# The last block of a mixture-of-experts layer is added by a gate matrix on TensorE instead of through DRAM

## The chip, the cores and the metric

One core of a Trainium2 chip runs the whole program. The metric is the device time of one execution in microseconds (us); lower is better. The engines are TensorE (PE), VectorE (DVE), ScalarE (ACT), GpSimd (POOL) and SyncE (SP); each takes its own instructions in order. Data between DRAM and on-chip memory moves through 16 DMA engines, which serve queues that SP, ACT and POOL issue to.

## The reference, cut to what matters

The program computes a block with four mixers and a dense feed-forward part, and behind it two layers, numbered 0 and 1 here. Each layer is a mixer, a layer norm, a mixture of experts and another layer norm. There are 32 experts of width 512 over 1024 features, and each token (512, in layer 0 with two more) takes its two best. The kernel's two steps behind the experts are

```python
gates = pg * jax.nn.softmax(vals, axis=-1)          # two gates for a token
...
xs = xpad[slot_tok].reshape(n_blocks, BLK, D)        # blocks of tokens of one expert
def expert_block(args):
    xb, e = args
    hb = jax.nn.silu(xb @ w_gate[e]) * (xb @ w_up[e])
    return hb @ w_down[e]
...
y = jnp.zeros((T + 1, D)).at[slot_tok].add(ys * slot_gate[:, None])
...
h = layer_norm(ALPHA * h + y, ln_g, ln_b)
```

## The kernel before

Each layer's mixture runs in one function. It routes the tokens, gathers them by expert from DRAM, and then takes 16 steps `u`, each a block of 128 rows that holds two experts (a pair). A step is `gate_up` (the two input products `peg`, then SiLU on ACT and a product on DVE), `hpose` (four transposes `pex` and a DVE copy), `down` (the output products `pey0`, `pey1`), and `scatter` (two ACT copies `eys<-pey`, then an indirect DMA from POOL that writes each row to the place of its token and choice in the DRAM array `dy`). `ORDER` is the order of the blocks; its last is block 15.

The experts' weights, 6 MB for an expert, are a stream: SP issues 1 MB DMAs into a ring of buffers `sr` as they come free. `items_moe` lays down their order. Behind one step's gate and up weights stand the down weights of the step before it, and the last step's down weights come at the very end: [gate and up of 15] [down of 14] [down of 15].

Behind the last step ACT scales the residual rows `xt` (in layer 0 also the two rows `hm`) by `ALPHA` (L2387). A loop for overfull experts follows (L2390); it has no rounds here, but all engines meet there. Then SP reads `dy` back by token (`cy<-dy`, 4 MB, L2418). The `COMBINE` string gives the order of the steps by token tile: S adds the two choices times their gates (two DVE instructions of 128x1024, L294 and L2423), N is the layer norm, G gain and bias (POOL L1620 and DVE L1621), T transposes the tile for the next mixer. In layer 0 the products `pl` of the short-convolution mixer follow; its weights `sc_w_in` are each split in two parts (ACT L222, DVE L224) in buffers `sh_*`. In layer 1 the tiles go to the output.

The order within each engine's queue around the experts is settled by a scheduler from the program, not by the text's order alone; the COMBINE part is under a manual order.

Of the kernel before, what the change touches and what calls it, by code (L numbers as in the profile page):

```python
# [46 lines left out]
NB = (NP + MORE + 1) // 2 * 2  # L47
CT = 32
GPC = ((640, 448, 640, 384, 448), (832, 832, 512, 320))
COMBINE = ("M4 S0 S1 N0 N1 S2 S4 N4 G0 G1 G4 T0 T1 T4 S3 N2 G2 N3 G3", "S0 S1 N0 S2 N1 S3 N2 G0 G1 N3 G2 G3")  # L50
MOE_W = ("moe_w_gate_2", "moe_w_up_2", "moe_w_down_2")
EPS = 1e-6
LN_EPS = 1e-5
# [1790 lines left out]
def items_moe(e, l):  # L1844


    def own(x):
        return lambda i: e.I[MOE_W[i]][l][x]

    def ranked(r):  # L1850
        return chosen(e, l, lambda: e.ranked(r))

    e.moe_first[l] = len(e.st.items)
    last = []
    for u in ORDER:
        pair = [own(x) for x in STAT[u]] if u < NST else [ranked(u), ranked(NE - 1 - u)]
        it = [p_ for pp in zip(*(expert_items(w) for w in pair)) for p_ in pp]
        n = len(it) * 2 // 3
        for i in it[:n] + last:
            e.st.add(*i)  # L1860
        last = it[n:]
    for i in last:
        e.st.add(*i)
# [168 lines left out]
def moe(e, mo):  # L2032
# [10 lines left out]
    with ExitStack() as ph:  # L2043
# [2 lines left out]
        xg = [sp.tile([P, D], F32, name=f"xg{i}") for i in range(2)]  # L2046
        for x_ in xg:
            G.memset(x_, 0.0)
        def small(name, shape, dt=F32):
            return sp.tile([P] + list(shape), dt, name=name)  # L2050

# [167 lines left out]
                                  q + k == 0, q + k == 2)  # L2219
            return pp  # L2220

        def scatter(po, yi):
            if not ysb:
                y2 = sp.tile([P, 2 * D], F32, name="eys")
                ysb.extend((y2[:, :D], y2[:, D:]))
            ys = ysb[0]
            ysb.rotate(1)
            for h in range(2):
                e.late = A.copy(ys[:, h * 512:(h + 1) * 512], po[h])  # L2229
            G.indirect_dma_start(out=dy[:, :], out_offset=bass.IndirectOffsetOnAxis(ap=yi, axis=0), in_=ys, in_offset=None,  # L2230
                                 bounds_check=2 * n_tok - 1, oob_is_err=False)

        def gates():

# [48 lines left out]
            V.tensor_copy(lst[:, :NL], pc_[:, 16:16 + NL])  # L2283
            V.tensor_copy(nov, pc_[:, 8:9])

        def block():

            b0 = sp.tile([P, 2], I32, name="ob0")
            ts(b0[:, 0:1], lst[:, 0:1], NE - 1, op0=OP.bitwise_and)
            ts(b0[:, 1:2], lst[:, 0:1], 5, op0=OP.arith_shift_right)  # L2290
            bf_ = sp.tile([P, 2], F32, name="obf")
            V.tensor_copy(bf_, b0)
            eo = sp.tile([P, NE], F32, name="oeo")
            ts(eo, mo.io, bf_[:, 0:1], op0=OP.is_equal)
# [21 lines left out]
            return ev, ox, oy  # L2316

        NL = 16
        gt = mo.gt
# [47 lines left out]
        def scatters(u, pp):  # L2367
            for b_, po in zip(work[u], pp):
                scatter(po, yix[:, b_:b_ + 1])

        get = lambda: st.raw_get(2)
        for u in range(NP):
            sg = gate_up(xs, get)
            if u + 1 < NP:
                xs = next_x(u + 1)
            if hs is not None:
                scatters(u - 1, down(hs, get))
            if u == 4:
                rows = mo.gain_bias(gb, l * 2 + 1)
                g, b = next(rows)  # L2380
            if u == NP - 2:
                next(rows)
            hs = [(hpose(x_), cut) for x_, cut in sg]
        scatters(NP - 1, down(hs, get))
        with tc.issue_after(e.late.ins):
            for h, n in rows_:
                A.activation(h, h, AF.Copy, scale=ALPHA)  # L2387
        if e.overflow:
            nv = nc.values_load(nov[0:1, 0:1], min_val=0, max_val=NL)
            with tc.For_i(0, nv, 1) as _:  # L2390
                ev, ox, oy = block()
# [9 lines left out]
                scatter(po, oy)  # L2401

    e.left = []
    if l == 0:
        e.xm.__exit__(None, None, None)
        e.act3 = tc.tile_pool(name="act3", bufs=1, side="right", reuse_waits="tile")
        e.open_act(e.act3.__enter__())
    with tc.tile_pool(name=f"cb{l}", bufs=1, reuse_waits="tile") as sp:
        order = [NT, 0, 1, 2, 3] if l == 0 else range(NT)
        ys = {}  # L2410
        with tc.manual_schedule(engines={mybir.EngineType.SP}):
            for t in order:
                if l == 0 and t == NT - 1:
                    st.stop()
                    st.prefetch()
                n = rows_[t][1]
                ys[t] = sp.tile([P, 2, D], F32, name="cy", bufs=4)
                Q.dma_start(ys[t][:n], dy[2 * t * P:2 * (t * P + n), :].rearrange("(t k) c -> t k c", k=2))  # L2418
        def sums(h, n, t):
            y_ = ys[t][:n]  # L2420
            stt(h, y_[:, 0, :], gt[:n, t, 0:1], h, OP.mult, OP.add)
            sm = sp.tile([P, 1], F32, name="csum", bufs=4)[:n]
            V.scalar_tensor_tensor(h, y_[:, 1, :], gt[:n, t, 1:2], h, op0=OP.mult, op1=OP.add, accum_out=sm)  # L2423
            return ln_sums(e, sp, h, n, [sm], y_[:, 0, :])

        def scaled(h, n, t):

            y_ = ys[t][:n]
            for k in range(2):
                A.activation(y_[:, k, :], y_[:, k, :], AF.Copy, scale=gt[:n, t, k:k + 1])  # L2430
                G.tensor_tensor(h, h, y_[:, k, :], op=OP.add)
            yield
            sm = sp.tile([P, 1], F32, name="msum")[:n]
            A.activation(y_[:, 0, :], h, AF.Identity, accum_out=sm)
            yield ln_sums(e, sp, h, n, [sm], y_[:, 0, :], "m")

        def step(c, t):
            h, n = rows_[t]
            if c == "M":
                ms[t] = scaled(h, n, t)  # L2440
                next(ms[t])
            elif c == "S":
                ms[t] = next(ms[t]) if t == NT else sums(h, n, t)
            elif c == "N":
                ln_norm(e, sp, h, n, *ms[t], "m" if t == NT else "")
            elif c == "G":
                ln_gain(e, h, n, g, b, GPC[l][t])
                if l == 1:
                    Q.dma_start(e.out[0, t * P:(t + 1) * P, :], h)
            else:  # L2450
                e.tile_to_fm(h, 2 + t * P if t < NT else 0, n)

        ms = {}
        with tc.manual_schedule(engines={mybir.EngineType.DVE, mybir.EngineType.Activation, mybir.EngineType.Pool}):
            t = order[0]
# [40 lines left out]
```

## Time and profile before

| | us |
|---|---|
| median of 3 runs | 2580.27 (2578.97 to 2581.33) |
| the profiled execution | 2577.17 |
| its span, first to last instruction | 2575.1 |

Times in the trace are microseconds from the start of the span. Layer 0's expert steps end with the last `pey` product at 1763.25, those of layer 1 at 2525.10. A row of a timeline has the start, the duration, the engine, the line and the operation, `out<-in`, how many were put together, and in brackets how long the engine had been idle and what ended that.

### The profile page before, as it was taken

Reading aid. Unit: us, or ns where it says so; the run is one execution under the profiler, and the core shown is the slowest. Engines: PE = TensorE matmul, PEld = TensorE weight load, DVE = VectorE, ACT = ScalarE, POOL = GpSimd, SP = SyncE. Lnnn points to the kernel's source line nnn. Section 1 sums busy time; section 2 is a strip of 40 time slices with the busy share of each in tenths; the row PEclk is TensorE's granted clock in tenths of the full one; section 3 lists DMA queues with packets and bytes.
Section 4 is the critical chain, followed back from the end, with each engine's and each line's share of the span. In section 5 each row is a group of like instructions: output and inputs, shape, how many; then the busy total and the mean of one; then the engine's idle time right before and its main releaser. Section 6 shows DMA issues by size and latency. Waiting matters only on the chain. (4 is left out here: it accounts for less than half of the span.)

```text
span 2575.1 us, 37407 instructions
## 1 busy us (share of the span) xinstructions
PE 2305.2 (90%) x15293; PEld 1475.1 (57%) x15293; DVE 939.0 (36%) x2127; ACT 666.8 (26%) x1062; POOL 238.5 (9%) x268
## 2 busy tenths in 40 slices
PE   7998999999999999999699899883999698899881
PEld 6886777887888888886532233221898432233220
DVE  4348878755533332665610000003544400000003
ACT  4335332123422222484200001013322100000012
POOL 0013130000100000100300000002101100000002
PEclk9999999999999999999699999997999699999996
DMA  4221221034223333325499999997226499999993
GB/s 141 91 79 43 87 70 63 22 99 168 69 88 98 98 131 99 91 69 196 152 370 420 420 414 416 412 418 263 69 83 239 160 411 419 418 414 414 414 405 120
DMA packets 176370, 556.85 MB, mean 216 GB/s; under 512 B 22216, under 2 KB 104870, under 8 KB 127042
## 3 DMA queue, kind: packets, MB, share of 16 engines
q1 hardware_dynamic: 154308, 523.29, 52.5%
q0 software_dynamic: 12768, 25.31, 2.7%
q10 hardware_dynamic: 9120, 5.83, 0.8%
q8 instruction: 122, 2.00, 0.3%
q14 instruction: 52, 0.43, 0.0%
HBM read 548.00 MB, written 25.21 MB: 223 GB/s over the span
## 5 line engine op out<-in xcount | busy, mean ns | idle before, releaser
L297 PE MATMUL peg<-sr,ext 128*32 128x512 f32 (+1 forms) x4064 | 527.0, 596 | 70.0 <-DMA sr<-in_moe_w_gate_dram 39.1
L297 PEld LDWEIGHTS peg<-sr,ext 128*32 128x32 f32 (+1 forms) x4064 | 142.2, 111 | 405.0 <-issue 271.4
L297 PE MATMUL pey<-sr,eh 128*32 128x512 f32 x1984 | 303.2, 597 | 14.9 <-DMA sr<-in_moe_w_down_dram 12.4
L297 PEld LDWEIGHTS pey<-sr,eh 128*32 128x32 f32 x1984 | 82.1, 110 | 194.8 <-issue 149.5
L282 DVE TENSOR_TENSOR eh<-eh,peg 128x512 f32<-128x512 f32 x34 | 23.4, 688 | 390.7 <-PE peg L297 390.7
L224 DVE TENSOR_TENSOR sh_0l<-sr,sh_0h 128x1024 fp32r<-128x1024 f32 x84 | 103.5, 1232 | 164.3 <-ACT sh_0h L222 163.7
L2229 ACT COPY eys<-pey 128x512 f32<-128x512 f32 x68 | 39.9, 586 | 430.1 <-PE pey L297 429.6
L222 ACT CAST sh_0h<-sr 128x1024 fp32r<-128x1024 f32 x84 | 88.1, 1048 | 238.7 <-PE pf L297 53.2
L2175 DVE COPY ext<-pex 128x512 f32<-128x512 f32 x34 | 23.4, 689 | 320.9 <-PE pex L316 320.9
L224 DVE TENSOR_TENSOR sh_1l<-sr,sh_1h 128x1024 fp32r<-128x1024 f32 (+1 forms) x65 | 77.4, 1191 | 105.4 <-ACT sh_1h L222 104.7
L224 DVE TENSOR_TENSOR sh_2l<-sr,sh_2h 128x1024 fp32r<-128x1024 f32 (+1 forms) x65 | 74.2, 1141 | 95.1 <-ACT sh_2h L222 94.8
L222 ACT CAST sh_1h<-sr 128x1024 fp32r<-128x1024 f32 (+1 forms) x65 | 66.5, 1023 | 146.7 <-PE pf L297 48.5
L222 ACT CAST sh_2h<-sr 128x1024 fp32r<-128x1024 f32 (+1 forms) x65 | 62.9, 967 | 152.3 <-PE pf L297 49.3
L2198 ACT ACTIVATE eh<-peg 128x512 f32<-128x512 f32 x34 | 20.3, 597 | 277.9 <-PE peg L297 277.9
L297 PE MATMUL pl<-hhi,sh_0h 128*128 128x264 f32 (+3 forms) x288 | 86.7, 301 | 1.8 <-ACT hhi L305 1.8
L297 PE MATMUL pl<-hlo,sh_0h 128*128 128x264 f32 (+3 forms) x288 | 86.3, 300 | 2.0 <-DVE hlo L306 2.0
L2230 POOL DMA_INDIRECT dy<-eys,yix x34 | 34.0, 999 | 575.8 <-ACT eys L2229 559.4
L297 PE MATMUL pl<-hhi,sh_0l 128*128 128x264 f32 (+3 forms) x288 | 86.0, 298 | 0.0
L2208 DVE COPY eh<-pex 128x512 f32<-128x512 f32 x34 | 23.3, 691 | 137.9 <-PE pex L316 137.9
L2165 POOL DMA_INDIRECT xg<-dh,tix x34 | 34.9, 1026 | 348.5 <-PE pex L316 271.9
L2175 ACT COPY ext<-pex 128x512 f32<-128x512 f32 x34 | 19.9, 586 | 172.3 <-PE pex L316 116.7
L297 PEld LDWEIGHTS pl<-hhi,sh_0h 128*128 128x128 f32 x288 | 55.2, 192 | 4.7 <-ACT hhi L305 2.5
(730 smaller groups left out, 4909.6 us busy)
## 6 DMA issues: line engine op xcount, KB each, us to landing
sr<-in_moe_w_gate_dram SPq DMA_DIRECT2D x128, 1024.0 KB
sr<-in_moe_w_up_dram SPq DMA_DIRECT2D x122, 1024.0 KB
sr<-in_moe_w_down_dram SPq DMA_DIRECT2D x122, 1024.0 KB
sr<-in_w_in_dram SPq DMA_DIRECT2D x34, 1024.0 KB
sr<-in_sc_w_in_dram SPq DMA_DIRECT2D x12, 1024.0 KB
sr<-in_ffn_w_gate_dram SPq DMA_DIRECT2D x11, 1024.0 KB
sr<-in_ffn_w_up_dram SPq DMA_DIRECT2D x11, 1024.0 KB
sr<-in_ffn_w_down_dram SPq DMA_DIRECT2D x10, 1024.0 KB
```

The costliest lines, as they stand in the source:

```text
L222: self.e.A.copy(hi, r)
L224: v.tensor_tensor(lo, r, f(hi), op=OP.subtract)
L282: V.tensor_tensor(out_, a, b, op=OP.mult)
L297: T.matmul(o, l, r, start=start, stop=stop)
L2165: G.indirect_dma_start(out=xg[i], out_offset=None, in_=dh[:, :], in_offset=bass.IndirectOffsetOnAxis(ap=ti, axis=0), bounds_check=n_tok - ...
L2175: (A.copy if k0 else V.tensor_copy)(x_[:, k0:k0 + 4, :].rearrange("p k c -> p (k c)"), pt)
L2198: A.activation(sg, pg, AF.Silu)
L2208: V.tensor_copy(hh.rearrange("p k c -> p (k c)"), pt)
L2229: e.late = A.copy(ys[:, h * 512:(h + 1) * 512], po[h])
L2230: G.indirect_dma_start(out=dy[:, :], out_offset=bass.IndirectOffsetOnAxis(ap=yi, axis=0), in_=ys, in_offset=None, bounds_check=2 * n_tok - ...
```

## The change

All of this is done in both layers.

- `dy` is filled with zeros at the start of the mixture (SP, nine or eight DMAs of 512 KB), since the last block no longer writes its rows there.
- The stream's order is changed for the last pair: [down of 14] [gate and up of 15] [down of 15].
- Block 14 is scattered as soon as its `down` is done. Then `shares` builds the matrix `gs` of block 15 (rows of the block by tokens, a gate where a row belongs to a token): DVE makes 128x128 pieces, TensorE transposes them (`pgs`), ACT copies them.
- `most` reads `dy` from POOL's queue, 512 KB in each DMA, into the `sh` buffers, and DVE adds them to the residual: eight additions of 128x1024 in layer 1, ten in layer 0 (two of them on the two rows `hm`).
- Block 15 goes through `down` and the copies to `eys`, and is not scattered. S is now two products `gs` by `eys` on TensorE (`pbt`) and two DVE additions of 128x512 from PSUM.
- The scaling by ALPHA and a load of `nov` stand at step 4 of the program, half of the gain's preparation at step 8. Layer 0's COMBINE has a new order, and its step M (the two rows on ACT and POOL) is gone.

```diff
-COMBINE = ("M4 S0 S1 N0 N1 S2 S4 N4 G0 G1 G4 T0 T1 T4 S3 N2 G2 N3 G3", "S0 S1 N0 S2 N1 S3 N2 G0 G1 N3 G2 G3")
+COMBINE = ("S0 S1 N0 S4 N1 G0 T0 N4 G1 T1 G4 T4 S2 S3 N2 N3 G2 G3", "S0 S1 N0 S2 N1 S3 N2 G0 G1 N3 G2 G3")
...
-        for i in it[:n] + last:
+
+        for i in (it[:n] + last if u != ORDER[-1] else last + it[:n]):
...
+        for r0 in range(0, 2 * n_tok, P):
+            n = min(P, 2 * n_tok - r0)
+            Q.dma_start(dy[r0:r0 + n, :], xg[1][:n])
...
+        idle = lambda i, x: st.hs[i][0].tile([P, D], F32, name=st.hs[i][1] + x)
+
+        def most():
+
+            for t, (h, n) in enumerate(rows_):
+                yy = [idle(t % 3, x) for x in "hl"]
+                for k, y_ in enumerate(yy):
+                    G.dma_start(y_[:n], dy[2 * t * P:2 * (t * P + n), :].rearrange("(t k) c -> t k c", k=2)[:, k, :])
+                for k, y_ in enumerate(yy):
+                    stt(h, y_[:n], gt[:n, t, k:k + 1], h, OP.mult, OP.add)
+
+        def shares(w, slot_, x):
+
+            gs = idle(3, x)
+            for t0 in range(0, nt, NT):
+                pt = bank("pgs")
+                for t in range(t0, min(nt, t0 + NT)):
+                    a_, b_ = [sp.tile([P, DE], F32, name="eh", bufs=3)[:, :P] for _ in range(2)]
+                    ts(a_, slot_, rk[:, 0, t:t + 1], w[:, 0, t:t + 1], OP.is_equal, OP.mult)
+                    ts(b_, slot_, rk[:, 1, t:t + 1], w[:, 1, t:t + 1], OP.is_equal, OP.mult)
+                    add(a_, a_, b_)
+                    tr(pt[:, (t - t0) * P:(t - t0 + 1) * P], a_)
+                n = min(NT * P, n_tok - t0 * P)
+                A.copy(gs[:, t0 * P:t0 * P + n], pt[:, :n])
+            return gs
+
+        def by_token(gs, ys, t):
+
+            n = rows_[t][1]
+            po = [bank("pbt") for _ in range(2)]
+            for h in range(2):
+                mm(po[h][:n], gs[:, t * P:t * P + n], ys[:, h * 512:(h + 1) * 512], True, True)
+            return [p_[:n] for p_ in po]
...
-            if u == NP - 2:
+                for h, n in rows_:
+                    A.activation(h, h, AF.Copy, scale=ALPHA)
+                nv = nc.values_load(nov[0:1, 0:1], min_val=0, max_val=NL)
+            if u == NP // 2:
                 next(rows)
             hs = [(hpose(x_), cut) for x_, cut in sg]
-        scatters(NP - 1, down(hs, get))
-        with tc.issue_after(e.late.ins):
-            for h, n in rows_:
-                A.activation(h, h, AF.Copy, scale=ALPHA)
+            if u == NP - 2:
+                scatters(u, down(hs, get))
+                hs = None
+                gs = shares(of_block(float(ORDER[-1]), u_), mo.slot, "h")
+                if l == 0:
+                    st.stop()
+        most()
+        (po,) = down(hs, get)
+        ylast = evict(po)
...
-    with tc.tile_pool(name=f"cb{l}", bufs=1, reuse_waits="tile") as sp:
-        order = [NT, 0, 1, 2, 3] if l == 0 else range(NT)
-        ys = {}
-        with tc.manual_schedule(engines={mybir.EngineType.SP}):
-            for t in order:
-                if l == 0 and t == NT - 1:
-                    st.stop()
-                    st.prefetch()
-                n = rows_[t][1]
-                ys[t] = sp.tile([P, 2, D], F32, name="cy", bufs=4)
-                Q.dma_start(ys[t][:n], dy[2 * t * P:2 * (t * P + n), :].rearrange("(t k) c -> t k c", k=2))
-        def sums(h, n, t):
-            y_ = ys[t][:n]
-            stt(h, y_[:, 0, :], gt[:n, t, 0:1], h, OP.mult, OP.add)
-            sm = sp.tile([P, 1], F32, name="csum", bufs=4)[:n]
-            V.scalar_tensor_tensor(h, y_[:, 1, :], gt[:n, t, 1:2], h, op0=OP.mult, op1=OP.add, accum_out=sm)
...
+            if c == "S":
+                sm = [lp.tile([P, 1], F32, name=f"csum{i}", bufs=4)[:n] for i in range(2)]
+                for i, p_ in enumerate(by_token(gs, ylast, t)):
+                    hh = h[:, i * 512:(i + 1) * 512]
+                    V.scalar_tensor_tensor(hh, p_, 1.0, hh, op0=OP.mult, op1=OP.add, accum_out=sm[i])
+                ms[t] = ln_sums(e, lp, h, n, sm, big(D)[:n])
...
-            e.table(AF.Sqrt, ys[t][:rows_[t][1], 0, 0:1])
+            e.table(AF.Sqrt, ylast[:, 0:1])
```
The order of the instructions on three engines follows, at the end of layer 1's experts. Brackets name what a row waits for: an engine, or `DMASW` for a DMA of POOL's queue and `DMAHW` for one of SP's.

On DVE, before, the last rows ahead of the loop are these. `eh<-eh,peg` is the product behind `gate_up`, `eh<-pex` the copy behind `hpose`; the last pair of the two is block 15's.

```order
L282 TENSOR_TENSOR eh_18670<-eh_18670,peg_18569 128x512 [waits PE_49,Activation_49]
L2208 COPY eh_18750<-pex_18745 128x512 [waits PE_49]
L282 TENSOR_TENSOR eh_18828<-eh_18828,peg_18753 128x512 [waits PE_49,Activation_49]
L2208 COPY eh_18875<-pex_18870 128x512 [waits PE_49]
L2389 TENSOR_LOAD nov_16057 [waits DVE_49]
L2390 COMPARE_AND_BRANCH
```
In the changed kernel DVE has, behind the copy of block 14's `hpose` and twelve rows of `shares`, the eight sums of `most` (from the buffers `sh3` and `sh1`) and then block 15's product and copy:

```order
L294 SCALAR_TENSOR_TENSOR xt_64<-sh3_0h_19082,gt_14330,xt_64 128x1024 [waits DMASW2_49]
L294 SCALAR_TENSOR_TENSOR xt_64<-sh3_0l_19083,gt_14330,xt_64 128x1024 [waits DMASW3_49,DVE_49]
L294 SCALAR_TENSOR_TENSOR xt_64<-sh1_2h_19088,gt_14330,xt_64 128x1024 [waits DMASW4_49]
L294 SCALAR_TENSOR_TENSOR xt_64<-sh1_2l_19089,gt_14330,xt_64 128x1024 [waits DMASW5_49,DVE_49]
L294 SCALAR_TENSOR_TENSOR xt_64<-sh1_1h_19094,gt_14330,xt_64 128x1024 [waits DMASW6_49]
L294 SCALAR_TENSOR_TENSOR xt_64<-sh1_1l_19095,gt_14330,xt_64 128x1024 [waits DMASW7_49,DVE_49]
L294 SCALAR_TENSOR_TENSOR xt_64<-sh3_0h_19100,gt_14330,xt_64 128x1024 [waits DMASW0_49]
L294 SCALAR_TENSOR_TENSOR xt_64<-sh3_0l_19101,gt_14330,xt_64 128x1024 [waits DMASW1_49,DVE_49]
L282 TENSOR_TENSOR eh_19072<-eh_19072,peg_19005 128x512 [waits PE_49,Activation_49]
L2212 COPY eh_19080<-pex_19075 128x512 [waits PE_49]
```
The eight sums, each pair of which waits for a DMA, are now ahead of block 15's product in the same queue. Layer 0 reads the same with ten sums.

On POOL, before, the last two scatters (of blocks 14 and 15) stand ahead of the loop:

```order
L2230 DMA dy_14149<-eys_16395,yix_16052 1024x1024 [waits DMASW0_49,Activation_49]
L2230 DMA dy_14149<-eys_16395,yix_16052 1024x1024 [waits DMASW1_49,Activation_49]
L2389 TENSOR_LOAD nov_16057 [waits DVE_49]
L2390 COMPARE_AND_BRANCH
L2390 ISA [waits DMASW4_49,DMASW3_49]
L2390 UNCONDITIONAL_BRANCH
```
In the changed kernel only those up to block 14's do, and the reads of `dy` stand behind it:

```order
L2237 DMA dy_14299<-eys_16553,yix_16210 1024x1024 [waits DMASW7_49,Activation_49]
L2237 DMA dy_14299<-eys_16553,yix_16210 1024x1024 [waits DMASW0_49,Activation_49]
L2248 DMA sh3_0h_19082<-dy_14299 128x1024 [waits DMASW1_49]
L2248 DMA sh3_0l_19083<-dy_14299 128x1024 [waits DMASW3_49]
L2248 DMA sh1_2h_19088<-dy_14299 128x1024
L2248 DMA sh1_2l_19089<-dy_14299 128x1024 [waits DMASW5_49]
L2248 DMA sh1_1h_19094<-dy_14299 128x1024
L2248 DMA sh1_1l_19095<-dy_14299 128x1024
L2248 DMA sh3_0h_19100<-dy_14299 128x1024 [waits DMASW2_49,DVE_49]
L2248 DMA sh3_0l_19101<-dy_14299 128x1024 [waits DMASW3_49,DVE_49]
```
The scatter of block 15 is gone, and eight reads have come in, the first behind a wait for a DMA of POOL's own queue. The last two of the rows wait for DVE as well, since they fill buffers that the first two sums empty.

On ACT, before, the last rows are block 15's copies and the scaling:

```order
L2229 COPY eys_16395<-pey0_18831 128x512 [waits DMASW7_49,PE_49,Activation_49]
L2229 COPY eys_16395<-pey1_18832 128x512 [waits PE_49,Activation_49]
L2229 COPY eys_16395<-pey0_18877 128x512 [waits DMASW0_49,PE_49,Activation_49]
L2229 COPY eys_16395<-pey1_18878 128x512 [waits PE_49,Activation_49]
L2387 ACTIVATE xt_64<-xt_64 128x1024 x4
```
In the changed kernel the load of a function table stands between the two copies:

```order
L2202 ACTIVATE eh_19072<-peg_19004 128x512 [waits DVE_49,PE_49]
L2233 COPY eys_16553<-pey0_19106 128x512 [waits DMASW0_49,PE_49,Activation_49]
L357 ACT_TABLE_LOAD
L357 ACTIVATE epst_69<-eys_16553,epst_69 128x1 [waits Activation_49]
L2233 COPY eys_16553<-pey1_19107 128x512 [waits PE_49]
L2432 TENSOR_LOAD nov_16215 [waits DVE_49]
L2446 COMPARE_AND_BRANCH
L2446 UNCONDITIONAL_BRANCH [waits Activation_49]
L2446 UNCONDITIONAL_BRANCH [waits barrier_Pool_Activation_PE_DVE_SP_release]
```
The scaling has left this place, and the second copy of block 15 has the table load and a small activation ahead of it.

## Rows read from the trace of the kernel before

**Rows 1.** Windows: busy us of each engine, TensorE's granted clock, DMA share, GB/s.
```profile
1260.00:1270.00 10.00, 0.94 (x8) 0.69 (x7) 9.04 (x42) 3.48 (x6) 0.00 (x0) 0.50 0.00 1
...
2030.00:2040.00 10.00, 1.85 (x8) 1.78 (x8) 9.31 (x43) 0.00 (x0) 0.00 (x0) 0.50 0.00 1
...
2300.00:2310.00 10.00, 10.00 (x90) 3.83 (x91) 1.98 (x3) 1.07 (x3) 1.13 (x2) 1.00 1.02 419
...
2500.00:2510.00 10.00, 8.95 (x72) 3.05 (x72) 1.38 (x2) 0.00 (x0) 0.00 (x0) 1.00 0.86 358
2510.00:2520.00 10.00, 8.94 (x68) 2.50 (x64) 0.00 (x0) 1.17 (x2) 0.98 (x1) 1.00 0.33 130
2520.00:2530.00 10.00, 4.03 (x26) 0.91 (x24) 0.00 (x0) 4.96 (x6) 0.98 (x1) 0.91 0.08 28
```
**Rows 2.** Timeline from the last step of layer 1 on.
```profile
2511.01 4.49 PE L297 MATMUL pey<-sr,eh 128*32 128x512 f32 x32 [0.57 <-SPq L2390]
...
2521.47 3.63 PE L297 MATMUL pey<-sr,eh 128*32 128x512 f32 x24 [1.06 <-DMA sr<-in_moe_w_down_dram]
...
2525.20 0.59 ACT L2229 COPY eys<-pey 128x512 f32<-128x512 f32 x1 [0.28 <-PEq L2390]
2525.68 3.89 ACT L2387 ACTIVATE xt<-xt 128x1024 f32<-128x1024 f32 x4
2526.05 0.98 POOL L2230 DMA_INDIRECT dy<-eys,yix  x1 [9.48 <-ACT eys L2229]
...
2530.91 1.28 ACT L357 ACT_TABLE_LOAD   x1 [1.34 <-issue]
...
2534.57 1.28 DVE L294 SCALAR_TENSOR_TENSOR xt<-cy,gt,xt 128x1024 f32<-128x1024 f32 x1 [27.55 <-DMA cy<-dy]
...
2543.93 4.97 POOL L1620 TENSOR_TENSOR xt<-xt,lngb 128x832 f32<-128x832 f32 x2 [16.90 <-ACT xt L1613]
...
2546.97 1.94 DVE L294 SCALAR_TENSOR_TENSOR lnrt<-lnrr,lnrv 128x1 f32<-128x1 f32 x1
```
**Rows 3.** Timeline from the last step of layer 0 to the mixer behind it.
```profile
1759.62 3.63 PE L297 MATMUL pey<-sr,eh 128*32 128x512 f32 x24 [1.07 <-SPq L2390]
...
1770.35 1.03 ACT L222 CAST sh_0h<-sr 128x1024 fp32r<-128x1024 f32 x1
...
1775.96 1.28 DVE L294 SCALAR_TENSOR_TENSOR xt<-cy,gt,xt 128x1024 f32<-128x1024 f32 x1
...
1789.16 3.14 POOL L1620 TENSOR_TENSOR xt<-xt,lngb 128x640 f32<-128x640 f32 x2 [6.44 <-ACT xt L1613]
...
1807.06 0.58 PE L297 MATMUL pl<-hhi,sh_0h 128*128 128x258 f32 x1
...
1811.05 0.42 PE L297 MATMUL pl<-hhi,sh_0h 128*128 128x258 f32 x1
...
1811.43 0.28 PE L297 MATMUL pl<-hhi,sh_0l 128*128 128x258 f32 x1
```
**Rows 4.** Timeline of POOL before the gathers of layer 0.
```profile
1255.38 1.86 POOL L2048 MEMSET xg<- 128x1024 f32 x2
```
**Rows 5.** DMA issues of the whole span: count, KB each, median us to landing.
```profile
dh<-xt POOLq DMA_DIRECT2D x8, 512.0 KB, 4.6
...
dy<-eys,yix POOLq DMA_INDIRECT x34, 8.3
```
**Rows 6.** DMA queues from 1243 to 1246: packets, MB, share of the engines.
```profile
q1 hardware_dynamic: 112, 0.87, 69.1%
q0 software_dynamic: 102, 0.41, 33.5%
```
**Rows 7.** Instructions grouped by line and shape, DVE, 1200 to 2576: count, busy, mean ns.
```profile
L282 DVE TENSOR_TENSOR eh<-eh,peg 128x512 f32<-128x512 f32 x34 | 23.4, 688 | 390.7 <-PE peg L297 390.7
L2208 DVE COPY eh<-pex 128x512 f32<-128x512 f32 x34 | 23.3, 691 | 137.9 <-PE pex L316 137.9
...
L1814 DVE SCALAR_TENSOR_TENSOR xt<-xt,pz 128x512 f32<-128x512 f32 x16 | 10.8, 681 | 6.7 <-PE pz L297 6.7
```

More of the change, by code (lines that the diff above doesn't have):

```diff
@@ L2220, in down, with evict @@
             return pp
-        def scatter(po, yi):
+        def evict(po):
             if not ysb:
@@ L2228, in scatter @@
             for h in range(2):
-                e.late = A.copy(ys[:, h * 512:(h + 1) * 512], po[h])
-            G.indirect_dma_start(out=dy[:, :], out_offset=bass.IndirectOffsetOnAxis(ap=yi, axis=0), in_=ys, in_offset=None,
+                A.copy(ys[:, h * 512:(h + 1) * 512], po[h])
+            return ys
+        def scatter(po, yi):
+            G.indirect_dma_start(out=dy[:, :], out_offset=bass.IndirectOffsetOnAxis(ap=yi, axis=0), in_=evict(po), in_offset=None,
                                  bounds_check=2 * n_tok - 1, oob_is_err=False)
+        idle = lambda i, x: st.hs[i][0].tile([P, D], F32, name=st.hs[i][1] + x)
[25 more added lines that the diff above has]
+            return [p_[:n] for p_ in po]
         def gates():
@@ L2284, in gates, with of_block @@
             V.tensor_copy(nov, pc_[:, 8:9])
+        def of_block(x, of):
+            w_ = sp.tile([P, 2, nt], F32, name="ow")
+            gk = gt.rearrange("p t k -> p k t")
+            stt(w_, of, x, gk, OP.is_equal, OP.mult)
+            return w_
         def block():
@@ L2307, in block @@
                 mm(po[:, 0:2], ro, s2[:, k, t, :], i_ == 0, i_ == 2 * nt - 1)
-            oy = sp.tile([P, 1], I32, name="ooy")
-            ts(oy, po[:, 0:1], -1.0, op0=OP.add)
             ox = sp.tile([P, 1], I32, name="oox")
-            ts(ox, oy, 1, op0=OP.arith_shift_right)
+            ts(ox, po[:, 0:1], -1.0, op0=OP.add)
+            ts(ox, ox, 1, op0=OP.arith_shift_right)
+            gs = shares(of_block(bb[:, 0:1], r), so, "l")
             ev = nc.values_load(b0[0:1, 0:1], min_val=0, max_val=NE - 1, engines=[mybir.EngineType.SP])
@@ L2315, in block @@
             V.tensor_copy(lst[:, 0:NL], ls2)
-            return ev, ox, oy
+            return ev, ox, gs
         NL = 16
@@ L2380, in moe @@
                 g, b = next(rows)
-            if u == NP - 2:
+                for h, n in rows_:
+                    A.activation(h, h, AF.Copy, scale=ALPHA)
+                nv = nc.values_load(nov[0:1, 0:1], min_val=0, max_val=NL)
+            if u == NP // 2:
                 next(rows)
             hs = [(hpose(x_), cut) for x_, cut in sg]
-        scatters(NP - 1, down(hs, get))
-        with tc.issue_after(e.late.ins):
-            for h, n in rows_:
-                A.activation(h, h, AF.Copy, scale=ALPHA)
+            if u == NP - 2:
[7 more added lines that the diff above has]
+        ylast = evict(po)
         if e.overflow:
-            nv = nc.values_load(nov[0:1, 0:1], min_val=0, max_val=NL)
             with tc.For_i(0, nv, 1) as _:
-                ev, ox, oy = block()
+                ev, ox, gv = block()
                 gather(0, ox)
@@ L2400, in moe @@
                 (po,) = down([(hpose(sg), P)], get)
[L2401 to L2407, printed above, removed]
-    with tc.tile_pool(name=f"cb{l}", bufs=1, reuse_waits="tile") as sp:
-        order = [NT, 0, 1, 2, 3] if l == 0 else range(NT)
-        ys = {}
-        with tc.manual_schedule(engines={mybir.EngineType.SP}):
-            for t in order:
-                if l == 0 and t == NT - 1:
-                    st.stop()
-                    st.prefetch()
-                n = rows_[t][1]
-                ys[t] = sp.tile([P, 2, D], F32, name="cy", bufs=4)
-                Q.dma_start(ys[t][:n], dy[2 * t * P:2 * (t * P + n), :].rearrange("(t k) c -> t k c", k=2))
-        def sums(h, n, t):
-            y_ = ys[t][:n]
-            stt(h, y_[:, 0, :], gt[:n, t, 0:1], h, OP.mult, OP.add)
-            sm = sp.tile([P, 1], F32, name="csum", bufs=4)[:n]
-            V.scalar_tensor_tensor(h, y_[:, 1, :], gt[:n, t, 1:2], h, op0=OP.mult, op1=OP.add, accum_out=sm)
[L2424 to L2435, printed above, removed]
@@ new lines, in moe @@
+                yv = evict(po)
+                for t, (h, n) in enumerate(rows_):
+                    for i, p_ in enumerate(by_token(gv, yv, t)):
+                        add(h[:, i * 512:(i + 1) * 512], h[:, i * 512:(i + 1) * 512], p_)
+        e.left = []
+        if l == 0:
+            e.xm.__exit__(None, None, None)
+            e.act3 = tc.tile_pool(name="act3", bufs=1, side="right", reuse_waits="tile")
+            e.open_act(e.act3.__enter__())
+            st.prefetch()
+        lp = ph.enter_context(tc.tile_pool(name=f"ln{l}", bufs=1, reuse_waits="tile"))
@@ L2437, in step @@
         def step(c, t):
             h, n = rows_[t]
[L2439 to L2443, printed above, removed]
+            if c == "S":
[4 more added lines that the diff above has]
+                ms[t] = ln_sums(e, lp, h, n, sm, big(D)[:n])
@@ L2444, in step @@
             elif c == "N":
-                ln_norm(e, sp, h, n, *ms[t], "m" if t == NT else "")
+                ln_norm(e, lp, h, n, *ms[t])
             elif c == "G":
@@ L2454, in moe @@
         with tc.manual_schedule(engines={mybir.EngineType.DVE, mybir.EngineType.Activation, mybir.EngineType.Pool}):
-            t = order[0]
-            e.table(AF.Sqrt, ys[t][:rows_[t][1], 0, 0:1])
+            e.table(AF.Sqrt, ylast[:, 0:1])
             for c in COMBINE[l].split():
```

## The prediction

> **What bounds the kernel now.** I read the windows first. In the expert steps the DMA share is 1.02 and some 419 GB/s arrive; TensorE also shows 10 of 10 us busy, but pipelined products fill a window whether or not they are late [rows 1]. The timeline decides between the two: before block 15's `down` TensorE waits for weights, and its two halves start 10.46 us after block 14's second one [rows 2], so 2 MB arrive every 5.23 us. The stream bounds both layers' expert steps, and at its end it runs out unevenly: 358, 130 and 28 GB/s in three windows, while the last weights come only at 2521.5 [rows 1, 2]. A few of the 16 DMA engines are late there, and the last product waits for them.
>
> Behind the stream comes a serial tail. In layer 1 the last `pey` product ends at 2521.47 + 3.63 = 2525.10 (call it T), the scatter is issued at 2526.05, and DVE's first sum starts at 2534.57, T + 9.5, after 27.55 us of waiting for `cy` [rows 2]. From there DVE, ACT and POOL hand the tiles on to the end of the span at 2575.1. In layer 0 T is 1759.62 + 3.63 = 1763.25; the first sum starts at T + 12.7, the first gain (POOL L1620) at T + 25.9, and the mixer's first product at T + 43.8 [rows 3]. So the change can act on two things: when T comes, and what follows it.
>
> **The change, part by part.**
>
> *Zeroing.* 4.2 MB written at some 418 GB/s are 10.0 us of DMA. They wait for the second `memset` of `xg`, which ends at 1257.24 [rows 4]; the DMA engines then move 1 GB/s or less in the windows shown (0.00 of their time), in either layer [rows 1]. The cover is the routing. Without it, it would be 10 us for each layer. I take 0.
>
> *ALPHA.* The four scalings take 3.89 us, but from T + 0.6 on, inside the wait for `cy` that ends at T + 9.5 [rows 2]: taking them away gives nothing. In routing they stand in front of copies on ACT; I take 0, at most 1 us.
>
> *T is later.* This is the large term, and it rests on the order on DVE: the sums of `most`, which wait for the reads of `dy`, stand ahead of block 15's product, behind which its transposes and `down` wait in turn. In layer 1, step by step:
>
> - Block 14's down weights take the place of block 15's gate weights, four halves of 5.23 us earlier than they are now: the second half at 2511.01 - 20.9 = 2490.1. The `pey` products end 4.5 later [rows 2], at 2494.6; the scatter is issued 1 us behind, as at T now, at 2495.5. It lands a median 8.3 us later [rows 5]: 2504. Then POOL issues the reads. Such a 512 KB DMA of POOL's queue lands after a median 4.6 us [rows 5]; data flow from about 2507.
> - The reads are 4.2 MB, spread over the same engines as the weights: 10.0 us more on each, the late ones included. From here to the end a late engine has 14.5 us of weights (2507 to 2521.5) and 10 us of `dy`, so it is done at 2531.5 whatever the order.
> - Which of the two lands last? Where POOL's queue and SP's stream ran side by side, they moved 102 and 112 packets, 0.41 and 0.87 MB [rows 6]: about equal turns, and a third of the bytes for POOL, whose packets are half as long. At a third, 10 us of `dy` would need 30 us beside the weights, so the weights land first (14.5 x 3/2: 2528.8) and `dy` lands last, at 2531.5.
> - Then come the last two sums, 2 x 1.30 by the 1.28 of such an instruction [rows 2], to 2534.1; block 15's product 0.69 and copy 0.69 [rows 7]; the four transposes between them, 1.1 (estimate; TensorE's clock is at half by then). `down` starts at 2536.6.
> - 64 products at 4.3 for 32 are 8.6 at full clock [rows 2]. After a rest, the half clock lasts: in layer 0 products of 258 columns still take 0.42 us at 1811.05, 4.0 us after the restart, and 0.28 at 1811.43 [rows 3]. With the transposes TensorE restarts at 2534.8, so until 2539.2 `down` is slow, which loses 1.5. T is 2546.7 in place of 2525.1: **+21.6**.
>
> In layer 0 the stream ends at 1759.6, the reads at 1759.6 + 10 + 0.8 (two small reads and the mixer's weights behind): 1770.4. Four sums follow (two on `hm`), 5.2, then as above 0.7 + 1.1 + 0.7 and 10.1: T is 1788.2 in place of 1763.25: **+24.9**.
>
> A formula of the Trainium skill speaks for much less ("DMA: Bandwidth & Descriptors", Anatomy of one DMA: 2.0 us and the bytes at 436 GB/s): one read by itself would take 3.2 us and all eight some 12, so they would land near 2516, about when block 15's product is due, and T would move by the 10 us on the late engines alone: 2585, as in the first rival below. The trace's own 4.6 us for 512 KB shows a queue that has to share, and nothing in the formula says how it fares beside a stream at share 1.02.
>
> *The tail is shorter, layer 1.* The scatter, its landing and the reload of `cy` go. In their place: the second `eys` copy, behind a table load of 1.28 [rows 2] and its small activation, ends at T + 2.0 instead of T + 0.7; the loop's meeting some 0.3 (estimate); the first `pbt` 0.6 to 0.9 (twice a 258-column product [rows 3]); two sums from PSUM, 0.76 each by the nearest shape, 0.68 [rows 7], and some 0.1 for the reading of its sum (estimate): the mean's input is there at T + 4.7. Before, it was at T + 9.5 + 2 x 1.3 = T + 12.1: -7.4. To the first gain, now at T + 18.8 [rows 2]: S1 is 1.1 shorter, but one more table load lies in between, +1.3: -7.2. S2 and S3 are 1.1 shorter each; but DVE's tiny `lnrt` takes 1.94 there and ends exactly with POOL's gain (2548.91 and 2548.90 [rows 2]), so an earlier DVE may only wait longer. Between -7 and -9.4; I take **-8**.
>
> *Layer 0.* The same start, T + 2.0, and a split of 1.03 [rows 3] before the meeting (the splits ran inside the wait for `cy`, a cover that goes): T + 3.4. ACT then has two table loads of 1.28 [rows 2], two splits of 1.03, and four DMA issues, two squares and a root (4.4, estimate): 9. DVE's five small steps and ACT's normalizing come to some 2.2 (estimate): the first gain at T + 15 to 16, now T + 25.9. From it to the mixer's first product is 17.9 now; S2 leaves this stretch, but its and S3's four `pbt`, some 3 us, and more work on DVE come in: 20. So T + 36 in place of T + 43.8: **-8**, between -4 (splits waiting) and -12.
>
> *The sum:* layer 0 +24.9 - 8 = +17; layer 1 +21.6 - 8 = +14; together **+31**. The profiled execution, 2577.2, becomes 2608; its 2580.3 median, which lies 3.1 above it, 2611. I forecast 2610.
>
> **Rivals.**
>
> - *Reads in time.* If `dy` gets more than 41% of a late engine (10 of 24.5 us), or starts some 10 us sooner, DVE is free by the time block 15's product is due. T then moves by the 10 us that the weights are late, +10 to +11 in each layer; with the tails -16: +5, about 2585. The equal turns speak against it [rows 6]. Chance 0.11.
> - *Faster: the reads fit into idle engines.* From 2500 to 2521.5 the stream leaves (420 - 358) x 10 + (420 - 130) x 10 us + (420 - 28) x 1.5 us, some 4.1 MB, unused [rows 1], which is just what `dy` needs. If the late engines' lag comes from their weights alone and `dy` goes through the early ones, T moves by 2 at most and the tails give 16: 2567. It decides whether the late engines carry a sixteenth of `dy` each: under 2 us of it there, this case wins. Against it: where POOL's and SP's queues met, their shares of the 16 engines add up to 1.03 [rows 6], so POOL's bytes had no engines to themselves. The Trainium skill says the same ("DMA: Bandwidth & Descriptors", Rules for kernel authors: spreading transfers over issuing engines doesn't help, for all run on the same 16). Chance 0.06.
> - *Worse.* If all of `down`, the `pbt` and the transposes run at half clock, and layer 0's splits wait behind one another, each layer loses 4 to 5 more: +40, 2620. Chance 0.12.
> - *The main case,* 0.71, has its own range of 2601 to 2619: layer 0's tail from -4 to -12, layer 1's from -7 to -9.4, and 2 us either way for when `dy` lands in each layer.
>
> **The numbers.** A measurement of this kernel tells 0.2%, 5 us, from no change. The range from 2584 to 2624 leaves out the faster case, a little of the reads in time, and the tip of the worst one. Faster takes the 0.06 and a little of the reads in time (a tail of -9 or -10 in both); the same is half of that case and the shallow end between it and the main one; the rest is slower: 0.08, 0.08, 0.84.
>
> **What would show it.** Right: eight (ten) sums L294 on DVE that wait for DMA, and right behind them block 15's product, with TensorE idle for over 10 us ahead of `pex`; T 20 to 26 us later against the step before; at the first sum from PSUM T + 3 in layer 1. Wrong, if the product finds its sums done, if T moves by 10 or less, if the windows of the routing lose DMA time to the zeroing, or if the mixer of layer 0 starts beyond T + 42.

## The result and the profile after

The changed kernel takes 2599.19 us (median of 4 runs, 2597.6 to 2600.57), the kernel before 2579.62 beside it (4 runs). The ratio is 1.0076, with a 95% interval from 1.0062 to 1.0090: slower by 19.6 us, inside the forecast range of 2584 to 2624 and 11 us below the forecast of 2610.

The timeline of the changed kernel at the end of layer 1, with the rows that answer to [rows 2]:

```profile
2512.38 0.97 POOL L2237 DMA_INDIRECT dy<-eys,yix  x1 [9.80 <-ACT eys L2233]
...
2520.61 0.57 POOL L2248 DMA_DIRECT2D sh_0h<-dy  x1 [7.26 <-DMA dy<-eys,yix]
...
2530.15 1.28 DVE L294 SCALAR_TENSOR_TENSOR xt<-sh_0h,gt,xt 128x1024 f32<-128x1024 f32 x1 [22.74 <-DMA sh_0h<-dy]
...
2531.24 5.32 PE L297 MATMUL peg<-sr,ext 128*32 128x512 f32 x28 [2.71 <-SPq L2446]
...
2546.56 1.28 DVE L294 SCALAR_TENSOR_TENSOR xt<-sh_1l,gt,xt 128x1024 f32<-128x1024 f32 x1 [1.92 <-DMA sh_1l<-dy]
...
2549.09 1.28 DVE L294 SCALAR_TENSOR_TENSOR xt<-sh_0l,gt,xt 128x1024 f32<-128x1024 f32 x1
2550.30 0.68 DVE L282 TENSOR_TENSOR eh<-eh,peg 128x512 f32<-128x512 f32 x1
...
2551.03 1.13 PE L316 MATMUL pex<-ident,eh 128*128 128x128 f32 x4 [14.47 <-DVE eh L282]
...
2552.99 8.48 PE L297 MATMUL pey<-sr,eh 128*32 128x512 f32 x64 [0.83 <-issue]
...
2561.31 1.28 ACT L357 ACT_TABLE_LOAD   x1
...
2564.84 0.69 DVE L2477 SCALAR_TENSOR_TENSOR xt<-pbt,xt 128x512 f32<-128x512 f32 x1 [11.95 <-PE pbt L297]
...
2573.64 3.95 POOL L1620 TENSOR_TENSOR xt<-xt,lngb 128x832 f32<-128x832 f32 x2 [36.11 <-ACT xt L1613]
...
2588.82 3.03 POOL L1620 TENSOR_TENSOR xt<-xt,lngb 128x320 f32<-128x320 f32 x2 [1.56 <-ACT xt L1613]
```
POOL issues block 14's scatter at 2512.38 and waits 7.26 us for it to land; the reads follow. DVE then stands in front of its first sum for 22.74 us, put down to the read. Block 15's second up product ends at 2531.24 + 5.32 = 2536.6, but its product on DVE starts only at 2550.30, right behind the last sum, and TensorE's idle time ahead of `pex`, 14.47 us, is put down to that product. So the row that the sums were put ahead of is the row that TensorE waits for. The last `pey` ends at 2552.99 + 8.48 = 2561.5, the new T of this layer, and the first sum from PSUM (DVE L2477) starts at 2564.84, T + 3.4.

In layer 0 the same wait is 21.52 us. Its timeline, with the rows that answer to [rows 3]:

```profile
1775.61 1.13 PE L316 MATMUL pex<-ident,eh 128*128 128x128 f32 x4 [21.52 <-DVE eh L282]
...
1777.57 8.78 PE L297 MATMUL pey<-sr,eh 128*32 128x512 f32 x64 [0.83 <-issue]
...
1792.07 3.73 ACTq L1956 DMA_DIRECT2D brt<-in_moe_b_group_dram  x1
...
1796.10 1.28 ACT L222 ACT_TABLE_LOAD   x1 [6.91 <-DMA brt<-in_moe_b_group_dram]
...
1805.66 3.14 POOL L1620 TENSOR_TENSOR xt<-xt,lngb 128x640 f32<-128x640 f32 x2 [15.57 <-ACT xt L1613]
```
The first gain (POOL L1620) starts 19.3 us behind the last `pey` (1777.57 + 8.78 = 1786.35) and the mixer's first product `pl` 40.5, where [rows 3] have 25.9 and 43.8. ACT is a part of why it is not sooner: of its 6.91 idle us ahead of the table load, 3.73 are the issue of one small load of routing constants.

For all comparisons below, the span is cut at events that every kernel has: the first gather `xg<-dh` of a layer, T (the end of its last `pey`), the first gain behind T, and, in layer 1, the end of the last gain on POOL. Each number is the difference of two starts or ends in the trace of that kernel's profiled execution, in us. "Behind" is the run with the sums behind the product, "SP" the one that also reads from SP, "table" the one that also moves the table load.

| | before | after | no reads, no sums | reads only | behind | SP | table |
|---|---|---|---|---|---|---|---|
| start to gather, layer 0 | 1280.7 | 1281.0 | 1286.6 | 1280.7 | 1284.3 | 1280.8 | 1283.9 |
| gather to T, layer 0 | 482.6 | 505.4 | 484.1 | 490.3 | 487.1 | 483.5 | 487.6 |
| T to first gain | 25.9 | 19.3 | 19.0 | 21.4 | 21.3 | 31.9 | 20.6 |
| T to the mixer's first product | 43.8 | 40.5 | 40.4 | 44.1 | 43.4 | 54.2 | 42.7 |
| from there to gather, layer 1 | 234.3 | 231.0 | 231.1 | 229.8 | 228.5 | 230.0 | 228.5 |
| gather to T, layer 1 | 483.7 | 503.6 | 483.8 | 491.0 | 491.4 | 484.0 | 491.9 |
| T to first gain | 18.8 | 12.2 | 12.2 | 13.9 | 13.9 | 20.5 | 12.4 |
| first to last gain | 21.0 | 18.2 | 18.2 | 18.2 | 18.2 | 18.2 | 18.2 |
| last gain to the end | 10.2 | 4.0 | 10.0 | 3.6 | 4.0 | 10.0 | 4.0 |

From before to after the span grows by 20.7: +22.8 and +19.9 until T in the two layers, -3.3 to the mixer and -3.3 more behind it in layer 0, -6.6 and -2.8 in layer 1's tail, -6.2 at the very end, and 0.3 ahead of it all. The first row shows something else: a stretch that the experiments leave as it is takes 1280.7 to 1286.6 us from one profiled execution to the next. From the second memset of `xg`, behind which the zeroing starts, to the gather it is 23.4 to 23.5 us in each of these kernels, so the difference lies ahead of the change. Single times of one kernel lie up to 11 us apart; whether for the same reason is open. So the parts are compared here as well as the sums.

### The profile page after: what moved, and what is told of

It is laid out like the page before. It is cut to its first block, busy times and chain, and to the rows that moved or that the text cites. A ratio compares the mean times of both kernels' runs of the same rounds, so it can differ in the third digit from the quotient of the medians.

```text
span 2595.8 us, 37597 instructions
## 1 busy us (share of the span) xinstructions
PE 2327.3 (90%) x15338; PEld 1482.7 (57%) x15338; DVE 956.8 (37%) x2186; ACT 669.5 (26%) x1065; POOL 237.4 (9%) x282
## 5 line engine op out<-in xcount | busy, mean ns | idle before, releaser
L297 PE MATMUL pey<-sr,eh 128*32 128x512 f32 x1984 | 297.4, 603 | 12.8 <-DMA sr<-in_moe_w_down_dram 11.0
L282 DVE TENSOR_TENSOR eh<-eh,peg 128x512 f32<-128x512 f32 x34 | 23.4, 687 | 347.2 <-PE peg L297 347.2
L2179 DVE COPY ext<-pex 128x512 f32<-128x512 f32 x34 | 23.4, 689 | 317.9 <-PE pex L316 317.9
L2212 DVE COPY eh<-pex 128x512 f32<-128x512 f32 x34 | 23.5, 691 | 127.7 <-PE pex L316 127.7
L2179 ACT COPY ext<-pex 128x512 f32<-128x512 f32 x34 | 19.9, 586 | 171.7 <-PE pex L316 115.5
L316 PE MATMUL pex<-ident,eh 128*128 128x128 f32 x136 | 26.8, 328 | 36.0 <-DVE eh L282 36.0
```

The costliest lines, as they stand in the source:

```text
L282: V.tensor_tensor(out_, a, b, op=OP.mult)
L297: T.matmul(o, l, r, start=start, stop=stop)
L316: T.transpose(o, i, ident[:n, :n])
L2179: (A.copy if k0 else V.tensor_copy)(x_[:, k0:k0 + 4, :].rearrange("p k c -> p (k c)"), pt)
L2212: V.tensor_copy(hh.rearrange("p k c -> p (k c)"), pt)
```

## The experiments

Each was built from the changed kernel, or from the kernel before where it says so. The ratio is to the kernel before, run on the same chip, with its 95% interval.

**The sums behind block 15's product.** Only the order on DVE changes; `e.hp` is the last copy of the transposes behind block 15's product.

```diff
-                for k, y_ in enumerate(yy):
-                    stt(h, y_[:n], gt[:n, t, k:k + 1], h, OP.mult, OP.add)
+                with tc.issue_after(e.hp.ins):
+                    for k, y_ in enumerate(yy):
+                        stt(h, y_[:n], gt[:n, t, k:k + 1], h, OP.mult, OP.add)
```

> The sums of the read-back rows are put behind block 15's product and copy on DVE; the reads themselves stay where they are. Theory of the order (T is late since DVE's queue holds block 15's product behind the sums): T comes 10 to 17 us sooner in each layer, limited by the last weights, and the time is 2565 to 2582. Rival, the transfers alone (the 4.2 MB of reads make the last weights so late that TensorE would wait for them anyway): T moves by under 3 us in each layer, and the time stays at 2593 to 2600.

Measured: 2572.46 (11 runs), ratio 0.9975 (0.9966 to 0.9984), 27 us below the changed kernel. T comes 18.3 us sooner in layer 0, a little more than forecast, and 12.2 in layer 1 (table). The timeline of layer 1's end:

```profile
2516.07 5.32 PE L297 MATMUL peg<-sr,ext 128*32 128x512 f32 x28 [2.72 <-SPq L2447]
...
2521.51 0.69 DVE L282 TENSOR_TENSOR eh<-eh,peg 128x512 f32<-128x512 f32 x1 [29.29 <-PE peg L297]
...
2522.26 0.75 PE L316 MATMUL pex<-ident,eh 128*128 128x128 f32 x4 [0.86 <-DVE eh L282]
...
2523.65 1.27 DVE L294 SCALAR_TENSOR_TENSOR xt<-sh_0h,gt,xt 128x1024 f32<-128x1024 f32 x1
...
2523.84 10.79 PE L297 MATMUL pey<-sr,eh 128*32 128x512 f32 x64 [0.83 <-issue]
...
2534.99 1.28 DVE L294 SCALAR_TENSOR_TENSOR xt<-sh_0l,gt,xt 128x1024 f32<-128x1024 f32 x1
...
2536.84 8.83 PE L297 MATMUL pbt<-eys,sh_0h 128*128 128x512 f32 x16 [2.21 <-ACTq L2447]
```
The product now follows the up products at once, TensorE is idle for 0.86 us ahead of `pex` instead of 14.47, and the sums run beside `down`. The order is shown to be the cause of most of the loss; the transfers alone are refuted as its whole. What is left of the lateness of T, 4.5 and 7.7 us, the next runs take up.

**Neither reads nor sums.** `most()` is left out.

> The reads and the sums are left out, so the outputs of all blocks but the last are missing. If reads and sums are the whole cost, T is where it is in the kernel before (within 2 us) and only the shorter tails are left: 2599 - 23 - 20 = 2556, between 2552 and 2560. If the gate matrix, the new order of the weights or the zeroing cost something too, 2562 or more.

Measured: 2567.67 (4 runs), ratio 0.9958 (0.9943 to 0.9973). The time is that of the second forecast, yet T is where the first has it: 484.1 and 483.8 us behind the gathers, against 482.6 and 483.7 before. So the gate matrix and the order of the weights make T at most 1.5 us later. What the profiled execution has above the first forecast is in the last row of the table, 10.0 instead of 4.0, which is taken up below, and in 5.6 us more ahead of the first gather.

**The reads alone.** The four lines of the sums are left out.

> The reads are made as in the changed kernel, the sums are left out, so the outputs of all blocks but the last are missing. Theory of the order: only the sharing of the DMA engines is left, T 5 to 10 us later than in the kernel before in each layer, 2566 to 2576. Rival, the transfers alone: as the changed kernel, 2593 to 2600. If the reads fit into idle engines: as without reads, 2552 to 2560.

Measured: 2573.13 (10 runs), ratio 0.9980 (0.9971 to 0.9990). T is 7.7 and 7.3 us later than before, as forecast. That is what the reads cost through the DMA engines with DVE out of the way (4.5 and 7.7 with the sums behind); their full 10 us do not show, and they are not free.

**Reads from SP, behind the weights.** On top of the sums behind:

```diff
-                    G.dma_start(y_[:n], dy[2 * t * P:2 * (t * P + n), :]...
+                    Q.dma_start(y_[:n], dy[2 * t * P:2 * (t * P + n), :]...
```

> As the run with the sums behind, and the reads are issued by SP, where they stand behind all weights of the layer, instead of by POOL beside them. If sharing the DMA engines is what still makes T 5 to 8 us late there, T is back within 2 us of the kernel before in each layer. The sums then wait for the reads instead, which end no sooner, and all engines meet behind the sums: the time stays within 4 us of the run with the sums behind, 2568 to 2577. If the reads' place cost the whole lateness, and nothing takes it over: 2558 to 2566.

Measured: 2583.09 (11 runs), ratio 1.0020 (1.0011 to 1.0029): slower than both forecasts. T is back (483.5 and 484.0), as both theories had it, but the sums end last and all engines wait for them:

```profile
2524.99 7.53 PE L297 MATMUL pey<-sr,eh 128*32 128x512 f32 x64 [0.83 <-issue]
...
2530.14 1.28 DVE L294 SCALAR_TENSOR_TENSOR xt<-sh_0h,gt,xt 128x1024 f32<-128x1024 f32 x1 [5.26 <-DMA sh_0h<-dy]
...
2539.13 1.28 DVE L294 SCALAR_TENSOR_TENSOR xt<-sh_0l,gt,xt 128x1024 f32<-128x1024 f32 x1
...
2540.92 9.24 PE L297 MATMUL pbt<-eys,sh_0h 128*128 128x512 f32 x16 [8.40 <-DVEq L2447]
...
2552.98 3.95 POOL L1620 TENSOR_TENSOR xt<-xt,lngb 128x832 f32<-128x832 f32 x2 [49.71 <-ACT xt L1613]
```
TensorE's first `pbt` waits 8.40 us, put down to DVE, and the first gain comes 20.5 us behind T instead of 13.9. So the lateness goes over from T to what follows, as forecast: from gather to first gain this order costs 7.0 us more than the sums behind alone in layer 0 (515.4 against 508.4) and nothing in layer 1 (504.5 against 505.3). Layer 0 has the mixer's weights in the same queue; whether that is the reason was not tried. A further 6.0 us are the end again.

**Routing constants from SP, on the changed kernel and on the mended one; the table load behind the second copy.**

```diff
-        A.dma_start(self.wr[:, :, 0:4], ...
+        (e.Q if l else A).dma_start(self.wr[:, :, 0:4], ...
...
-            e.table(AF.Sqrt, ylast[:, 0:1])
+            e.table(AF.Sqrt, ylast[:, D - 1:D])
```

The first hunk stands for four loads of the same form. The expectations are, in order, of the constants on the changed kernel, the constants on the mended one (sums behind), the table load on the mended one, and both there.

> The four small loads of layer 1's routing constants are issued by SP instead of ACT, where they stand 6 us long behind the meeting of the engines and ahead of layer 0's tail. If they hold up that tail: layer 0's first gain comes 4 to 6 us sooner, 2593 to 2596. If DVE or the splits hold it anyway: 2597 to 2600.

> As the run with the sums behind, and the four loads of layer 1's routing constants are issued by SP instead of ACT. On the changed kernel this brought layer 0's first gain 2.2 us closer to T, which its time, with 10 us between its runs, could not show. Here the same 2 to 3 us: 2568 to 2571. If the meeting behind the sums hides it: as the run with the sums behind, 2571 to 2574.

> As the run with the sums behind, and the table load on ACT reads the second half of the copied block, so it stands behind the second copy instead of between the two. If the copy is on the path: 1.3 to 1.6 us sooner in each layer, 2569 to 2570. If the sums, or the load of the next weights, end last before the engines meet: no change, 2571 to 2574.

> The sums behind block 15's product, the table load behind the second copy, and the routing constants issued by SP, all three. The table load gave 0.7 us in layer 0 and 1.5 in layer 1 by the traces, the constants 1.3 in layer 0: 2568 to 2571, 7 to 10 us below the kernel before. If SP's four loads hold up the mixer's weights behind them: 2571 to 2575.

Measured: on the changed kernel 2599.25 (5 runs, 2593.8 to 2603.38), the first gain 17.1 us behind T instead of 19.3; on the mended one 2574.80 (11 runs, ratio 0.9986, 0.9977 to 0.9995), above both forecasts, the first gain 1.3 us sooner. The traces show these 2.2 and 1.3 us, the times show no gain. The table load: 2570.94 (9 runs), ratio 0.9971 (0.9960 to 0.9981), between its two forecasts, first gain 1.5 us sooner in layer 1 and 0.7 in layer 0. Both together: 2570.98 (9 runs), ratio 0.9974 (0.9964 to 0.9984). The constants are worth nothing that can be measured. The table load is worth 0.7 and 1.5 us by the traces; the times, 0.9971 against 0.9975, do not tell it from nothing. The lowest time of a kernel that leaves nothing out, sums behind and table moved, is 7 us below the kernel before.

**The end of the program.** In the kernel before, the last gain ends 10.2 us ahead of the end, in the changed one 4.0. Most of what lies there in the kernel before is the last long instruction in POOL's queue, a drain, which all engines wait for. The rows of that line in the two kernels (count; minimum, median and maximum in ns; first and last start), before:

```profile
L2492 POOLq DRAIN  x3: 46/115/10752, 2563.5 to 2574.9; - x3
```
and after:

```profile
L2526 POOLq DRAIN  x3: 46/115/2175, 2590.4 to 2595.2; - x3
```
10.75 us against 2.18. In both it starts 1.5 us before the last gain ends (2561.93 + 3.03 = 2564.96 and 2588.82 + 3.03 = 2591.85), so about that much of each is the gain. It is 8.6 us shorter and the end only 6.2, for in the changed kernel SP then still waits 2.1 us for the last DMA of the output. It was short in every run with POOL's reads and long in the two without. Four variants of the kernel before, with small plain reads added on POOL's queue, look for the reason; the diff is that with 16, the others have 1, 1 (held behind the last scatter) and 8:

```diff
+        if l == 1:
+            for i in range(16):
+                G.dma_start(small(f"tiny{i}", [1]), dh[0:P, 0:1])
```

> The kernel before with one plain 512-byte read added on POOL's queue behind the last scatter of layer 1; its result is not used. POOL's last drain took 10.8 us in the kernel before and 10.6 in the run without reads, where POOL's last DMA is an indirect one, and 2.2 in the three runs whose last is a plain one. If the kind of the last DMA sets it: a drain of 2 to 3 us and 5 to 7 us off the time, 2571 to 2574. If it is something else in the changed kernel: 10 to 11 us, and the time of the kernel before, 2577 to 2580.

> The kernel before with the plain 512-byte read of layer 1 kept behind the last scatter in POOL's queue (in the run before this one it had moved 500 us ahead, so that run could not tell). The drain was 10.6 to 10.8 us in all four kernels whose last DMA of POOL is indirect and 2.2 in all four whose last is plain. If the kind of the last DMA sets it: a drain of 2 to 3 us and 5 to 7 us off the time of the kernel before, 2571 to 2574. If not: 10 to 11 us and no change.

> The kind of the last DMA is refuted. What orders all drains so far is the number of DMAs that POOL issued: 10.59 us at 111, 10.75 at 113, 10.83 at 114 (0.08 each) and 2.18 at 129, as if the count began anew somewhere between. Here the kernel before gets 16 plain 512-byte reads on POOL's queue in layer 1's routing, where POOL is idle, which makes 129; their results are not used. If the count sets it: a drain of 2 to 3 us, 8 us off the time of the kernel before, 2568 to 2572. If it is the size or the place of the reads of the changed kernel: a drain of 10 to 12 us, and no change.

> The same with 8 reads, 121 DMAs of POOL. If the count begins anew at 120 or before: a drain of 1.5 to 2 us and 2568 to 2572. If between 122 and 129: 11.4 us by the slope of 0.08, and the time of the kernel before or 0.6 more.

Measured, in this order: one read that stood far ahead of the last scatter, 2577.51 (11 runs), ratio 1.0004 (0.9995 to 1.0013), drain 10.83; one read kept behind the last scatter, 2578.44 (11 runs), ratio 1.0003 (0.9994 to 1.0012), drain 10.84, so the kind of the last DMA does not set it; 16 reads, 2573.24 (11 runs), ratio 0.9980 (0.9971 to 0.9989), drain as the count has it and the time 1.2 us above its forecast; 8 reads, 2579.87 (11 runs), ratio 1.0006 (0.9997 to 1.0015), drain as forecast, time 1.9 us above the kernel before, where 0.6 at most was forecast. The same row in the run with 16 reads:

```profile
L2495 POOLq DRAIN  x3: 46/115/2175, 2564.9 to 2570.0; - x3
```
and in that with 8:

```profile
L2495 POOLq DRAIN  x3: 46/115/11403, 2566.6 to 2578.5; - x3
```
POOL issues 113 DMAs in the kernel before (all of them counted in the trace), 111 without the reads, 114 with one more, 121 with 8 and 129 with 16, as in the changed kernel. The drain takes 10.59, 10.75, 10.83, 11.40 and 2.18 us: 0.08 more for each DMA from 111 to 121, direct or indirect, and a fall somewhere between 122 and 129. In the profile of the run with 16 reads the end is 4.0 us as in the changed kernel, and the first gain of layer 1 comes 20.5 us behind T instead of 18.8, which takes back 1.7 of the gain. Where exactly the drain falls, whether it then grows again, and why, was not tried.

## Why the prediction was right, point by point

- **The order on DVE**, the step on which all rested, held: sums that wait for reads, then the product, then TensorE. In layer 1 the product was forecast to start at 2534.1 in the clock of the kernel before; it started at 2550.30, and with the 16.5 us by which that layer's gather is later, that is 2533.8. `down` was due at 2536.6 and came at 2552.99 - 16.5 = 2536.5. T moved by +22.8 and +19.9 against +24.9 and +21.6. The run with the sums behind shows that it was this order.
- **How POOL and SP share** was mis-sized, without harm. From 2530 to 2535 the changed kernel's queues stand so:

```profile
q0 software_dynamic: 306, 1.12, 56.7%
q1 hardware_dynamic: 124, 0.87, 42.0%
```
POOL has 57% of the engines' time and more packets than SP, not the equal turns of [rows 6], and from 2521 to 2546.6 the two moved 4.15 and 4.13 MB, where a third was forecast for POOL. The reads landed last all the same: six stand behind one another in POOL's queue, the first lands 9.5 us after its issue and the sixth 23.2; the eighth, issued at 2537.00 into a buffer that a sum had emptied, lands 12.0 us later, at 2549.0. In the clock of the kernel before that is 2532.5, against the 2531.5 of the forecast, which added both streams up on a late engine and did not hang on their shares. That some of the 16 engines are late stays an estimate, for the traces show only their mean. The formula of the Trainium skill ("DMA: Bandwidth & Descriptors", Anatomy of one DMA: 2.0 us and the bytes at 436 GB/s) gives 3.2 us for one such read by itself (estimate). In layer 1 none landed in less than 9.5.
- **`down` at half clock** was the term of T that was too large: 10.1 us forecast, 8.48 measured in layer 1 and 8.78 in layer 0. (In layer 0 the product also came 1.0 us sooner than forecast, at 1774.89.) The windows of the changed kernel show that the clock was low as forecast (PEclk is the column ahead of the last two):

```profile
2550.00:2555.00 5.00, 3.14 (x16) 1.44 (x20) 1.67 (x3) 0.00 (x0) 0.00 (x0) 0.50 0.01 2
2555.00:2560.00 5.00, 5.00 (x46) 1.65 (x42) 0.00 (x0) 0.00 (x0) 0.00 (x0) 0.92 0.00 0
```
The 64 products take 7.53 us in the run without reads, where nothing holds them and the granted clock is 1.00, and not the 8.6 that was read from rows that include waits for weights. The low clock, up to 2555.8 by the 0.92, costs 1 us (8.48 - 7.53) and not 1.5.
- **The zeroing** was taken at nothing, and costs nothing that shows: from the second memset of `xg` to layer 0's gather are 23.4 us in both kernels, and from the last products of the routing (`plg`) to layer 1's gather 19.7 in both (2021.72 to 2041.39 before, 2038.22 to 2057.89 after).
- **Layer 1's tail**: -7.2 to the first gain was forecast, -6.6 measured; behind it 0 to -2.2, measured -2.8.
- **Layer 0's tail**: -8 was forecast up to the mixer's first product, -3.3 measured. The term that failed most is ACT's four DMA issues: 1790.82 to 1796.08, 5.3 us, where they were counted with some 1.6. Off ACT, they brought the first gain only 2.2 us closer, so the rest of its lateness (T + 19.3 against T + 15 to 16) is open. Another 3.3 came back between the mixer's first product and layer 1's gather, which nothing in the forecast speaks of, so that the layer as a whole was right by luck (+17 forecast, +16.2 measured); why that stretch gains was not tried.
- **The end** was missing from the sum: -6.2 us in a drain that nothing in the forecast speaks of (the change has POOL issue 16 DMAs more). With T's 3.8 it is most of the 11 us between forecast and result.
- **The rivals.** Reads in time: its condition, more than 41% for `dy`, was met in the window above, and DVE was not free. Block 15's product was due when the up weights were through, at 2536.6, and not with the last weights of the stream, so 41% was too little for that case. With DVE out of the way T is 4.5 to 7.7 us late, where it had 10 to 11. Reads that fit into idle engines: refuted by the run with the reads alone, where T is over 7 us late and not 2. Worse by 40: the span grew by 20.7.

The change is not a bad idea with a bad price: mended, it beats the kernel before by 0.25%, and by 0.29% with the table load moved. But most of that is the drain: the kernel before with 16 idle reads is 0.20% faster by itself, and the 0.05 to 0.09% between them are within the intervals. By the table, the mended kernel saves 13.9 us behind T apart from the end, and the reads beside the weights take 12.2 of them back ahead of it.

## What to carry to other kernels

Read the order of each engine's queue, not the text of the program: a scheduler had moved work that waits for DMA ahead of the one instruction that TensorE needed, and taking it back was worth 27 us. A read that takes no time on a path may still lengthen a saturated stream, so look at which engine or queue it leaves late, and cost the end of the program too.

## What the hardware showed that was not expected

POOL's drain at the program's end grew by 0.08 us with each DMA that POOL had issued, 10.59 us at 111 to 11.40 at 121, and was 2.18 at 129; why is open. Sixteen reads of 512 bytes that nobody uses made the kernel before 4.7 us faster (ratio 0.9980, 0.9971 to 0.9989). Packets of two queues did not take equal turns once the reads ran: 306 of POOL's against 124 of SP's in 5 us, and 102 against 112 in [rows 6].
